# Grouping of the output projection's passes, the ring of raw tiles and the order of the first MLP unit in a hybrid attention and RWKV-7 encoder layer

## The chip, the cores and the metric

The kernel runs on one core of a Trainium2 chip. The core has five engines with an instruction stream each: TensorE (PE, matrix products; its weight loads are listed as PEld), VectorE (DVE), ScalarE (ACT), GpSimd (POOL) and SyncE (SP, which here issues DMA transfers). They wait for one another by semaphores. The metric is the time on the device in microseconds, as the median of several executions.

## What is computed

One encoder layer on x of 1024 positions by 1024 features in float32. The change lies behind the attention and the RWKV part, in the last two lines:

```python
x = x + jnp.concatenate([attn, rwkv], axis=-1) @ w_out[layer]
h = _rms_norm(x, ln2_g[layer])
x = x + jnp.square(jax.nn.relu(h @ w_up[layer])) @ w_down[layer]
```

`w_out` is 1024 x 1024, `w_up` 1024 x 4096 and `w_down` 4096 x 1024.

## The kernel before, in words

All of it stands in `tail`. Data lies with features on the 128 partitions and positions along the free axis, so x is eight tiles `x1[c]` of 128 x 1024, and a half `hf` of one is 128 x 512. Float32 products are made of three matmuls: each operand is split into a high part (a cast by ACT) and a low part (a subtraction by DVE), in `split_w` (L101, L102), and `mm3` (L105, L106, L107) issues high times high, high times low and low times high into one PSUM tile.

**Output projection.** `w_out(ks, c)` loads the weight blocks of column block c for the input tiles ks (`w2raw`), splits them (`w2h`, `w2l`), and for both halves runs three matmuls for each tile of ks and adds the result to x1[c] on DVE (L1026). Input tiles 4 to 7 are RWKV outputs (`rw`), 0 to 3 attention outputs (`f`). Tile 3 is written in place by the last attention pair, while tiles 0 to 2 are loaded back by `cat` from DRAM (`catr`) and split. There are three passes over the eight column blocks: [4, 5, 6, 7], interleaved with the last pieces of attention, then [0, 1], then [2, 3].

**Making h.** Inside the last pass each finished x1[c] becomes `hraw` (L1059, ACT). The norm's scale by position is applied later, after the up layer. The up layer multiplies 2 x 2 blocks with seven products in place of eight, so that for each pair of column blocks seven quadrants are made, 11, 21, 22 as they are and T1 to T4 from differences `ht` (L1067, L1068, L1071, L1072), each split into a high (L1056, ACT) and a low part (L1057, DVE).

**Up layer.** Sixteen units of two w_up tiles (`wuraw`, 512 KB each). `factors` forms the seven weight combinations, with sums on POOL (`wus`, L1099), and splits each (`wuh`, `wul`); `up_unit` runs a product of twelve matmuls for each and adds outputs on DVE (L1152). `sums` squares x1 on ACT (L1120, `sqt`) and adds on POOL (L1121) into `rep`; `scales` turns that into the norm's factor through PE (`psr`, L1126), a square root on ACT, a reciprocal on DVE and PE again (`psb`, L1132); `finish` applies factor, relu and square (L1168, L1169) and stores to `f_dr` (L1170).

**Down layer.** Four groups of eight `f_dr` tiles, each loaded in halves (`fraw`) and split (`mh`, `ml`); for each column block the weights (`wdraw`, two of 256 KB) are split (`wdh`, `wdl`), and 48 matmuls follow.

**What sets the order.** A scheduler orders the instructions of each engine by a priority that grows along the code, while every tile pool gives out a fixed number of buffers, and a tile that takes an old buffer's place waits until its readers are done. `ahead(n)` lets pieces of code take an earlier priority: the attention pieces of `some(4)` are such. On every engine instructions run strictly in the order so made.

## Time and profile before

| | us |
|---|---|
| median of 3 runs | 1776.54 |
| lowest, highest | 1776.28, 1782.05 |
| the profiled execution | 1780.65 |
| its span, first to last instruction | 1778.6 |
| output projection, from its first matmul (979.85) to its last | 95 |
| from there to the first matmul of unit 1 | 55 |
| units 1 to 15 | 286 |
| down layer with its start | 358 |

The profile is of one execution, so its times are set against its own 1780.65 us. A page lists busy time by engine, groups of like instructions with the mean of one, and what ended the idle time ahead of them; a timeline lists single instructions with start and length in microseconds; a table of windows gives busy time and count for each engine in stretches of time.

### The profile page before, as it was taken

The numbers are of one execution on the slowest core, as the hardware profiler recorded it, in microseconds if no ns is written. First come the engines' busy times: TensorE is split into PE (matmuls) and PEld (weight loads), VectorE is DVE, ScalarE is ACT, GpSimd is POOL, SyncE is SP. The second block draws the span as 40 slices with busy tenths as digits, with TensorE's granted clock in tenths as the row PEclk, the third lists the DMA queues.
The fourth block names the chain that finished last, engine by engine and source line by source line (L and its number), as shares of the span: only waits on it lengthen the run. The fifth ranks groups of instructions, "written<-read, shape, count | busy, mean of one in ns | idle before, by whom it ended". The sixth has DMA issues, their size and how long they took to land.

```text
span 1778.6 us, 30157 instructions
## 1 busy us (share of the span) xinstructions
PE 1622.7 (91%) x11720; PEld 1342.5 (75%) x11720; DVE 1031.8 (58%) x1946; ACT 596.9 (34%) x1091; POOL 424.5 (24%) x462
## 2 busy tenths in 40 slices
PE   7999978979869998988998994999999899999999
PEld 5777767767757777877786883888888788888887
DVE  6655657747545323565776578778878662424221
ACT  5544333443412213434465336222222251212110
POOL 3022022222200000221223117766666500000000
PEclk9999988879889997888998996999999999999999
DMA  6155787889875598998873411232232381413121
GB/s 220 46 143 129 155 166 154 174 178 187 190 172 142 170 231 194 270 264 228 228 219 108 155 36 36 83 131 101 103 128 101 105 268 49 141 63 110 48 96 52
DMA packets 347805, 256.67 MB, mean 144 GB/s; under 512 B 239984, under 2 KB 293120, under 8 KB 343568
## 3 DMA queue, kind: packets, MB, share of 16 engines
q1 hardware_dynamic: 311280, 212.60, 46.0%
q0 software_dynamic: 8704, 26.78, 5.0%
q10 hardware_dynamic: 27680, 15.38, 3.3%
q8 instruction: 92, 1.51, 0.4%
q14 instruction: 49, 0.40, 0.1%
HBM read 167.00 MB, written 87.69 MB: 143 GB/s over the span
## 4 chain that ended last, share of the span: by engine, by line
PE 67%; DMA 13%; DVE 9%; SPq 4%; issue 3%; ACT 3%; POOL 1%; ACTq 0%; DVEq 0%; POOLq 0%
PE ps L105 13%; PE ps L107 13%; PE ps L106 13%; PE ps_u L107 3%; PE ps_u L106 3%; PE ps_u L105 3%; DMA v_dr<-vn 2%; PE pvb L748 2%; DMA rec_dr<-G 2%; PE psd L564 2%; PE psg L496 1%; DMA ql<-ql_dr 1%; PE ps_pt L742 1%; DMA rec<-rec_dr 1%; DMA t<-td 1%
## 5 line engine op out<-in xcount | busy, mean ns | idle before, releaser
L105 PE MATMUL ps<-mh,wdh 128*128 128x512 f32 x512 | 199.5, 391 | 6.8 <-ACT wdh L101 6.8
L106 PE MATMUL ps<-ml,wdh 128*128 128x512 f32 x512 | 200.0, 391 | 0.0
L107 PE MATMUL ps<-mh,wdl 128*128 128x512 f32 x512 | 199.5, 391 | 0.0
L105 PE MATMUL ps_u<-hh,wh 128*128 128x512 f32 x368 | 156.3, 425 | 3.5 <-DVE ur L308 3.5
L107 PE MATMUL ps_u<-hh,wl 128*128 128x512 f32 x368 | 151.4, 411 | 0.0
L106 PE MATMUL ps_u<-hl,wh 128*128 128x512 f32 x368 | 150.7, 410 | 0.0
L1204 DVE TENSOR_TENSOR x<-x,ps 128x512 f32<-128x512 f32 x64 | 43.9, 686 | 150.0 <-PE ps L107 150.0
L105 PEld LDWEIGHTS ps<-mh,wdh 128*128 128x128 f32 x512 | 96.8, 189 | 27.2 <-ACT wdh L101 7.2
L107 PEld LDWEIGHTS ps<-mh,wdl 128*128 128x128 f32 x512 | 96.7, 189 | 20.3
L101 ACT CAST wdh<-wdraw 128x512 fp32r<-128x512 f32 x64 | 39.7, 622 | 215.3 <-PE ps L106 209.7
L106 PEld LDWEIGHTS ps<-ml,wdh 128*128 128x128 f32 x512 | 96.7, 189 | 20.0
L105 PEld LDWEIGHTS ps_u<-hh,wh 128*128 128x128 f32 x368 | 72.5, 197 | 20.2 <-DVE ur L308 4.3
L107 PEld LDWEIGHTS ps_u<-hh,wl 128*128 128x128 f32 x368 | 72.3, 197 | 17.7 <-issue 1.6
L106 PEld LDWEIGHTS ps_u<-hl,wh 128*128 128x128 f32 x368 | 72.2, 196 | 16.3 <-issue 2.4
L101 ACT CAST wuh<-wus 128x512 fp32r<-128x512 f32 x64 | 39.6, 622 | 128.9 <-PE ps L106 120.3
L102 DVE TENSOR_TENSOR wdl<-wdraw,wdh 128x512 fp32r<-128x512 f32 x64 | 44.0, 688 | 57.4 <-ACT wdh L101 57.3
L102 DVE TENSOR_TENSOR wul<-wus,wuh 128x512 fp32r<-128x512 f32 x64 | 67.9, 1062 | 12.1 <-ACT wuh L101 10.5
L496 PE MATMUL psg<-al,bk 64*128 64x128 f32 x512 | 56.8, 318 | 19.2 <-DVE G L501 10.6
L496 PEld LDWEIGHTS psg<-al,bk 64*128 64x128 f32 x512 | 48.0, 216 | 26.9 <-issue 11.9
L705 DVE CUSTOM_DVE_ANT_0 sb<-ps_s,bias 128x256 f32<-128x256 f32 (+1 forms) x136 | 50.0, 403 | 30.6 <-PE ps_pt L719 24.6
L1169 POOL TENSOR_TENSOR zz<-zz 128x512 f32<-128x512 f32 x48 | 57.4, 1195 | 35.3 <-DVE zz L1168 35.3
L102 DVE TENSOR_TENSOR wul<-wuraw,wuh 128x512 fp32r<-128x512 f32 x48 | 61.3, 1277 | 3.5 <-ACT wuh L101 1.9
(408 smaller groups left out, 4045.7 us busy)
## 6 DMA issues: line engine op xcount, KB each, us to landing
...
wuraw<-in_w_up SPq DMA_DIRECT2D x32, 512.0 KB, 4.2
fraw<-f_dr SPq DMA_DIRECT2D x64, 256.0 KB, 3.7
wdraw<-in_w_dn SPq DMA_DIRECT2D x64, 256.0 KB, 2.5
f_dr<-zz POOLq DMA_DIRECT2D x48, 256.0 KB, 2.5
raw<-in_w_in SPq DMA_DIRECT2D x46, 256.0 KB, 3.1
...
rec_dr<-G SPq DMA_DIRECT2D x32, 256.0 KB, 4.4
```

What stands on the lines that cost most here:

```text
L101: nc.scalar.copy(hi, raw)
L102: nc.vector.tensor_sub(lo, raw, r2f(hi))
L105: nc.tensor.matmul(ps, lh, rh, start=start, stop=False)
L106: nc.tensor.matmul(ps, lh, rl, start=False, stop=False)
L107: nc.tensor.matmul(ps, ll, rh, start=False, stop=stop)
L496: nc.tensor.matmul(pss[h][:, c], bk[H[h], 4 * g + c, h:h + 2].rearrange("p a b -> p (a b)"), al[H[h], 4 * g + c].rearrange("p a b -> p (a ...
L564: nc.tensor.matmul(ps[H[h], c], L[H[h], c], R[H[h], c], start=True, stop=True)
L705: nc.vector.tensor_tensor_reduce(sb[rows, i, :n], ps[rows, i, cols], b[rows], -1.0, 3.0e38, ALU.add, ALU.min, O[rows, js][:, i, mc:mc + 1])
L742: nc.tensor.transpose(pt[:, x, i * P:(i + 1) * P], sb[:, i, x * P:(x + 1) * P], ident)
L748: nc.tensor.matmul(pv[:, i], pts[:, x, i * P:(i + 1) * P], vB[:, x * 4 + c], start=(x == 0), stop=(x == 1))
L1169: nc.gpsimd.tensor_mul(t, t, t)
L1204: nc.vector.tensor_add(x1[c][:, HS[hf]], x1[c][:, HS[hf]], ps)
```

## The change

The passes become [4, 5, 6, 7], [0] and [1, 2, 3]: the middle one has half the matmuls that it had and the last one half as many again. All raw tiles of 128 x 1024 (attention tiles, w_up, f_dr, w_down) come from one ring `raw4` of two buffers, three from the up layer on, and the split weights of both MLP layers from one pool `wu` that lasts. The first two w_up tiles are loaded before the last pass. t2 is made by POOL instead of DVE, and the differences have two buffers instead of three. Unit 0 takes its products in the order 11, 21, 22, T2, T3, T1, T4; every other unit keeps 11, T2, T3, T1, 21, T4, 22. `sums` stands behind unit 0 in the code, with half of its additions on DVE, and the weights of the down layer's first column block are loaded and split ahead of that layer. Line numbers behind the change are some 11 to 31 higher.

```diff
+            wr = st.enter_context(tc.tile_pool(name="wr", bufs=2, side="right", reuse_waits="tile"))
             out = ExitStack()
-            c23 = out.enter_context(tc.tile_pool(name="c23", bufs=1, side="right", reuse_waits="tile"))
-            wp = out.enter_context(tc.tile_pool(name="wp3", bufs=4, side="right", reuse_waits="tile"))
+            c13 = out.enter_context(tc.tile_pool(name="c13", bufs=1, side="right", reuse_waits="tile"))
+            wp = out.enter_context(tc.tile_pool(name="wp3", bufs=2, side="right", reuse_waits="tile"))
+            wp.tile([P, 384], F32, name="rest4", bufs=1)
...
-            parts = [[c01.tile([P, S], F32R, name=f"f{i}{k}") for k in range(2)] +
-                     [c23.tile([P, S], F32R, name=f"f{i}{k}") for k in (2, 3)] +
+            o0 = ExitStack()
+            c00 = o0.enter_context(tc.tile_pool(name="c00", bufs=1, side="right", reuse_waits="tile"))
+            w0 = o0.enter_context(tc.tile_pool(name="w0", bufs=3, side="right", reuse_waits="tile"))
+            parts = [[(c13 if k else c00).tile([P, S], F32R, name=f"f{i}{k}") for k in range(4)] +
                      [rw[i][:, p] for p in range(4)] for i in range(2)]
             fh, fl = parts
+            pools, turn = [(wr, "raw4")] * 2, [0]
+
+            def raw4(src):
+                pool, tag = pools[turn[0] % len(pools)]
+                turn[0] += 1
+                r = pool.tile([P, NK, P], F32, name="raw4", tag=tag)
+                nc.sync.dma_start(r, src)
+                return r
...
+                raw = raw4(cat_dr[k].rearrange("p (k m) -> p k m", m=P)).rearrange("p k m -> p (k m)")
                 for hf in range(2):
-                    raw = wp.tile([P, 512], F32, name="catr", bufs=2)
-                    nc.sync.dma_start(raw, cat_dr[k][:, HS[hf]])
-                    split_w(raw, fh[k][:, HS[hf]], fl[k][:, HS[hf]])
-
-            def w_out(ks, c):
-                ws = []
-                for k in ks[::2]:
-                    raw = wp.tile([P, 2, P], F32, name="w2raw")
-                    nc.sync.dma_start(raw, w_o[c][:, k:k + 2])
-                    ws.append([wp.tile([P, 2, P], F32R, name=n) for n in ("w2h", "w2l")])
-                    split_w(raw, *ws[-1])
+                    split_w(raw[:, HS[hf]], fh[k][:, HS[hf]], fl[k][:, HS[hf]])
...
+            def w_out(wp, ks, c):
+                ws = {}
+                for i in range(0, len(ks), 3 if len(ks) == 3 else 2):
+                    k = ks[i]
+                    n = len(ks) if len(ks) < 4 else 2
+                    raw = wp.tile([P, n, P], F32, name="w2raw", bufs=3)
+                    nc.sync.dma_start(raw, w_o[c][:, k:k + n])
+                    w = [wp.tile([P, n, P], F32R, name=x) for x in ("w2h", "w2l")]
+                    split_w(raw, *w)
...
-                w_out([4, 5, 6, 7], c)
+                w_out(w0, [4, 5, 6, 7], c)
...
-                w_out([0, 1], c)
-            o01.close()
+                w_out(w0, [0], c)
...
-            rep = hp.tile([P, S], F32, name="rep3")
+            raws = {f: raw4(w_up[f]) for f in (0, 1)}
             with tc.tile_pool(name="ht", bufs=2, side="right", reuse_waits="tile") as ht:
                 for c in range(NK):
-                    w_out([2, 3], c)
+                    w_out(wp, [1, 2, 3], c)
...
-                    t1, t2, t3, t4 = (ht.tile([P, 512], F32, name=f"ht{i}", tag="ht", bufs=3) for i in range(4))
+                    t1, t2, t3, t4 = (ht.tile([P, 512], F32, name=f"ht{i}", tag="ht") for i in range(4))
                     nc.gpsimd.tensor_sub(t1, he[:, HS[1]], he[:, HS[0]])
-                    nc.vector.tensor_sub(t2, h[:, HS[1]], t1)
+                    nc.gpsimd.tensor_sub(t2, h[:, HS[1]], t1)
...
-            wu = up_.enter_context(tc.tile_pool(name="wu", bufs=4, side="right", reuse_waits="tile"))
+            wu = st.enter_context(tc.tile_pool(name="wu", bufs=4, side="right", reuse_waits="tile"))
+            wr3 = st.enter_context(tc.tile_pool(name="wr3", bufs=1, side="right", reuse_waits="tile"))
+            pools.append((wr3, "raw5"))
+            zu = up_.enter_context(tc.tile_pool(name="zu", bufs=5, side="right", reuse_waits="tile"))
+            rep = zu.tile([P, S], F32, name="rep3", bufs=1)
...
-                    r = wu.tile([P, NK, P], F32, name="wuraw", bufs=3)
-                    nc.sync.dma_start(r, w_up[f])
+                    r = raws.pop(f) if f in raws else raw4(w_up[f])
...
+                yield halves(a11)
+                if u == 0:
+                    yield halves(a12)
                 s1 = summed(nc.gpsimd.tensor_add, a21, a22)
                 s2 = summed(nc.gpsimd.tensor_sub, s1, a11)
-                yield parts(s2)
-                yield parts(summed(nc.gpsimd.tensor_sub, a11, a21))
-                yield parts(s1)
-                yield parts(a12)
-                yield parts(a22)
-                yield parts(summed(nc.gpsimd.tensor_sub, a12, s2))
+                if u == 0:
+                    yield halves(summed(nc.gpsimd.tensor_sub, a12, s2))
+                yield halves(s2)
+                yield halves(summed(nc.gpsimd.tensor_sub, a11, a21))
+                yield halves(s1)
+                if u > 0:
+                    yield halves(a12)
+                yield halves(a22)
+                if u > 0:
+                    yield halves(summed(nc.gpsimd.tensor_sub, a12, s2))
 
...
-                        t = wu.tile([P, 512], F32, name="sqt", tag="z")
+                        t = zu.tile([P, 512], F32, name="sqt", tag="z")
                         nc.scalar.activation(t, x1[c][:, sl], AF.Square)
-                        nc.gpsimd.tensor_add(rep[:, sl], rep[:, sl], t)
+                        (nc.gpsimd if hf else nc.vector).tensor_add(rep[:, sl], rep[:, sl], t)
...
+                if u == 0:
+                    z11, = add([t1], "21", [z("z")])
+                    p3 = acc()
+                    prod(p3, "22")
+                    c3 = z("z")
+                    nc.scalar.copy(c3, p3)
                 U2, = add([t1], "T2", [z("u", bufs=1)])
                 U3, = add([U2], "T3", [z("t3", bufs=1)])
                 z22, V = add([U3, U2], "T1", [z("z"), z("z")])
-                z11, = add([t1], "21", [t1])
-                z21, = add([U3], "T4", [z("z")])
-                z12, = add([V], "22", [V])
+                if u > 0:
+                    z11, = add([t1], "21", [t1])
+                z21, = add([U3], "T4", [z("z") if u else U3])
+                if u > 0:
+                    z12, = add([V], "22", [V])
+                else:
+                    z12 = V
+                    nc.vector.tensor_add(V, V, c3)
...
+            first = up_unit(0)
             sums()
-            first = up_unit(0)
             scales()
...
+            def dn(g, c):
+                r = raw4(w_dn[g, c])
+                return [halves(r[:, 4 * j:4 * j + 4]) for j in range(2)]
+            ws = dn(0, 0)
             up_.close()
...
-            wd = st.enter_context(tc.tile_pool(name="wd", bufs=4, side="right", reuse_waits="tile"))
...
+                    raw = raw4(f_dr[g * 8 + f].rearrange("p (k m) -> p k m", m=P)).rearrange("p k m -> p (k m)")
                     for hf in range(2):
-                        raw = wd.tile([P, 512], F32, name="fraw")
-                        nc.sync.dma_start(raw, f_dr[g * 8 + f][:, HS[hf]])
-                        split_w(raw, hi[:, HS[hf]], lo[:, HS[hf]])
+                        split_w(raw[:, HS[hf]], hi[:, HS[hf]], lo[:, HS[hf]])
...
-                    ws = []
-                    for j in range(2):
-                        raw = wd.tile([P, 4, P], F32, name="wdraw")
-                        nc.sync.dma_start(raw, w_dn[g, c][:, 4 * j:4 * j + 4])
-                        ws.append([wd.tile([P, 4, P], F32R, name=n) for n in ("wdh", "wdl")])
-                        split_w(raw, *ws[-1])
+                    if g + c:
+                        ws = dn(g, c)
```

On SP, the stretch that ends in the loads of x1, before (cat_dr_91 is attention tile 2 in DRAM):

```order
L1018 DMA w2raw<-in_w_o 128x256 x4
L1011 DMA catr<-cat_dr_89 128x512 x2
L1018 DMA w2raw<-in_w_o 128x256 x4
L836 DMA cat_dr_91<-aT 128x512
L896 DMA bon<-bon_dr 128x4x128
L895 DMA gt<-g_dr 128x4x128
L836 DMA cat_dr_91<-aT 128x448
L836 DMA cat_dr_91<-aT 128x64
L1030 DMA x_0_10313<-in_xT 128x1024
```

and now:

```order
L1010 DMA raw_10712<-cat_dr_89 128x1024
L1010 DMA raw_10718<-cat_dr_90 128x1024
L836 DMA cat_dr_91<-aT 128x512
L896 DMA bon<-bon_dr 128x4x128
L895 DMA gt<-g_dr 128x4x128
L836 DMA cat_dr_91<-aT 128x448
L836 DMA cat_dr_91<-aT 128x64
L1010 DMA raw_10724<-cat_dr_91 128x1024
L1010 DMA raw_10922<-in_w_up 128x1024
L1029 DMA w2raw<-in_w_o 128x256 x3
L1029 DMA w2raw<-in_w_o 128x384
L1042 DMA x_0_10313<-in_xT 128x1024
```

The eight early loads of w2raw moved behind the load of attention tile 2 and that of the first w_up tile.

On ACT, from the last h quadrant to the norm's square root, before (wuh are weights of units 0 and 1):

```order
L1056 CAST hT4h_10955<-ht_11239 128x512
L1120 ACTIVATE sqt<-x_1_10314 128x512 x2
L1120 ACTIVATE sqt<-x_2_10315 128x512 x2
L1120 ACTIVATE sqt<-x_3_10316 128x512
L101 CAST wuh<-wuraw 128x512
L1120 ACTIVATE sqt<-x_3_10316 128x512
L1120 ACTIVATE sqt<-x_4_10317 128x512 x2
L1120 ACTIVATE sqt<-x_5_10318 128x512
L1157 COPY zt<-ps_11338 128x512
L1120 ACTIVATE sqt<-x_5_10318 128x512
L101 CAST wuh<-wus 128x512 x3
```

and now, where the casts of a11 and a12 stand further up:

```order
L1068 CAST hT4h_10909<-ht_11244 128x512
L1178 COPY zt<-ps_11306 128x512
L1138 ACTIVATE rep_11273<-x_0_10313 128x512 x2
L101 CAST wuh<-wus 128x512 x4
L101 CAST wuh<-raw_10924 128x512
L1184 COPY zz<-ps_11344 128x512
L101 CAST wuh<-raw_11529 128x512
L101 CAST wuh<-wus 128x512 x2
L1141 ACTIVATE sqt<-x_1_10314 128x512
L101 CAST wuh<-wus 128x512
L1141 ACTIVATE sqt<-x_1_10314 128x512
L1141 ACTIVATE sqt<-x_2_10315 128x512 x2
```

The squares moved from ahead of unit 0's weights to behind all of them and four of unit 1's.

On DVE, from the last output of the up layer into the down layer, before:

```order
L1152 TENSOR_TENSOR zz<-zz,ps_13841 128x512
L1168 SCALAR_TENSOR_TENSOR zz<-zz,rep_10968 128x512
L102 TENSOR_TENSOR ml_13882<-fraw,mh_13881 128x512 x2
L102 TENSOR_TENSOR ml_13892<-fraw,mh_13891 128x512 x2
L102 TENSOR_TENSOR wdl<-wdraw,wdh 128x512 x3
L102 TENSOR_TENSOR ml_13902<-fraw,mh_13901 128x512
L102 TENSOR_TENSOR wdl<-wdraw,wdh 128x512
```

and now:

```order
L1173 TENSOR_TENSOR zt<-zt,ps_13814 128x512
L102 TENSOR_TENSOR wul<-raw_13883,wuh 128x512
L1200 SCALAR_TENSOR_TENSOR zt<-zt,rep_11273 128x512
L1173 TENSOR_TENSOR zz<-zt_13772,ps_13833 128x512
L1200 SCALAR_TENSOR_TENSOR zz<-zz,rep_11273 128x512
L1173 TENSOR_TENSOR zz<-zz,ps_13851 128x512
L1200 SCALAR_TENSOR_TENSOR zz<-zz,rep_11273 128x512
L102 TENSOR_TENSOR ml_13899<-raw_13900,mh_13898 128x512 x2
L102 TENSOR_TENSOR ml_13907<-raw_13908,mh_13906 128x512 x2
```

The low part of the first down weights moved into the last unit, while the low parts of all f tiles stay behind its last output.

More of the change, by code (lines that the diff above doesn't have):

```diff
@@ L1008, in cat @@
             def cat(k):
+                raw = raw4(cat_dr[k].rearrange("p (k m) -> p k m", m=P)).rearrange("p k m -> p (k m)")
                 for hf in range(2):
[L1010 to L1020 removed]
+                    split_w(raw[:, HS[hf]], fh[k][:, HS[hf]], fl[k][:, HS[hf]])
[8 more added lines that the diff above has]
+                    split_w(raw, *w)
+                    for z in range(n):
+                        ws[k + z] = w[0][:, z], w[1][:, z]
                 for hf in range(2):
@@ L1023, in w_out @@
                     for i, k in enumerate(ks):
[L1024 to L1025 removed]
+                        mm3(ps, *ws[k], fh[k][:, HS[hf]], fl[k][:, HS[hf]], i == 0, i == len(ks) - 1)
                     nc.vector.tensor_add(x1[c][:, HS[hf]], x1[c][:, HS[hf]], ps)
@@ L1036, in tail @@
             for c in range(NK):
-                w_out([0, 1], c)
-            o01.close()
+                w_out(w0, [0], c)
+            o0.close()
             left.close()
@@ L1079, in acc, with halves @@
                 return pu.tile([P, 512], F32, name=name, tag="acc")
-            wu = up_.enter_context(tc.tile_pool(name="wu", bufs=4, side="right", reuse_waits="tile"))
+            wu = st.enter_context(tc.tile_pool(name="wu", bufs=4, side="right", reuse_waits="tile"))
[3 more added lines that the diff above has]
+            rep = zu.tile([P, S], F32, name="rep3", bufs=1)
             f_dr = [dr.tile([P, S], F32, name=f"f_dr{f}") for f in range(32)]
+            def halves(src):
+                w = [wu.tile([P, 4, P], F32R, name=n) for n in ("wuh", "wul")]
+                split_w(src, *w)
+                return w
             def factors(u):
@@ L1086, in factors @@
                 for f in (2 * u, 2 * u + 1):
-                    r = wu.tile([P, NK, P], F32, name="wuraw", bufs=3)
-                    nc.sync.dma_start(r, w_up[f])
+                    r = raws.pop(f) if f in raws else raw4(w_up[f])
                     raw.append(r.rearrange("p (k e) m -> p e k m", e=2))
                 a11, a12, a21, a22 = raw[0][:, 0], raw[0][:, 1], raw[1][:, 0], raw[1][:, 1]
-                def parts(src):
-                    w = [wu.tile([P, 4, P], F32R, name=n) for n in ("wuh", "wul")]
-                    split_w(src, *w)
-                    return w
                 def summed(fn, x, z):
-                    t = wu.tile([P, 4, P], F32, name="wus", bufs=3)
+                    t = zu.tile([P, 4, P], F32, name="wus", bufs=3)
                     fn(t, x, z)
                     return t
-                yield parts(a11)
+                yield halves(a11)
+                if u == 0:
+                    yield halves(a12)
                 s1 = summed(nc.gpsimd.tensor_add, a21, a22)
                 s2 = summed(nc.gpsimd.tensor_sub, s1, a11)
-                yield parts(s2)
-                yield parts(summed(nc.gpsimd.tensor_sub, a11, a21))
-                yield parts(s1)
-                yield parts(a12)
-                yield parts(a22)
-                yield parts(summed(nc.gpsimd.tensor_sub, a12, s2))
+                if u == 0:
[8 more added lines that the diff above has]
+                    yield halves(summed(nc.gpsimd.tensor_sub, a12, s2))
             def sums():
@@ L1145, in z @@
                 def z(tag, **kw):
-                    return wu.tile([P, 512], F32, name=f"z{tag}", tag=tag, **kw)
+                    return zu.tile([P, 512], F32, name=f"z{tag}", tag=tag, **kw)
                 def add(a, q, out):
```

4 lines of the change are left out of this document (removed).

## The prediction

> **What bounds the kernel now.** I read the first part of the page and its costliest groups first, then a table of windows over the last 800 us, then the timeline at the idle places that the table shows.
>
> ```profile
> PE 1622.7 (91%) x11720; PEld 1342.5 (75%) x11720; DVE 1031.8 (58%) x1946; ACT 596.9 (34%) x1091; POOL 424.5 (24%) x462
> ...
> 979.30:1008.00 28.70, 28.70 (x159) 24.61 (x158) 16.43 (x35) 10.12 (x25) 0.00 (x0) 1.00 0.51 179
> ...
> 1057.30:1075.30 18.00, 17.75 (x74) 13.02 (x72) 17.68 (x26) 13.88 (x23) 8.67 (x6) 1.00 0.01 1
> 1075.30:1096.20 20.90, 0.12 (x1) 0.00 (x0) 19.62 (x23) 13.59 (x23) 12.53 (x9) 0.56 0.09 27
> 1096.20:1131.00 34.80, 29.30 (x117) 23.57 (x118) 20.18 (x22) 13.31 (x22) 28.65 (x21) 0.79 0.17 60
> 1131.00:1417.20 286.20, 286.20 (x1260) 236.65 (x1259) 226.10 (x268) 70.83 (x117) 183.19 (x181) 1.00 0.31 108
> 1417.20:1424.00 6.80, 0.05 (x1) 0.00 (x0) 3.99 (x6) 2.47 (x4) 2.57 (x3) 0.88 0.82 255
> 1424.00:1431.00 7.00, 6.95 (x20) 5.60 (x21) 5.34 (x8) 4.30 (x8) 0.00 (x0) 0.63 1.02 375
> 1431.00:1778.60 347.60, 343.89 (x1518) 284.51 (x1516) 117.93 (x180) 69.75 (x116) 0.00 (x0) 1.00 0.30 98
> ```
>
> Columns: length, then busy time and count of PE, PEld, DVE, ACT, POOL, then granted clock, DMA share and GB/s. PE is full in every stage that the change touches but two: 21 us after the output projection, where DVE is busy for 19.6 of 20.9, with a slow first unit behind it, and 7 us ahead of the down layer, where the DMA share is 0.82. Only those two places have something to give. In between, 1260 matmuls in 286.2 us, the first few of them slow, make 0.2267 us each: a product of 12 is 2.72 us, a unit of 84 is 19.0.
>
> ```profile
> 1075.02 0.40 PE L107 MATMUL ps<-f,w2l 128*128 128x512 f32 x1
> ...
> 1092.12 3.63 SPq L1088 DMA_DIRECT2D wuraw<-in_w_up  x3
> ...
> 1093.16 1.76 DVE L1057 TENSOR_TENSOR hT4l<-ht,hT4h 128x512 fp32r<-128x512 f32 x1
> ...
> 1095.56 0.62 ACT L101 CAST wuh<-wuraw 128x512 fp32r<-128x512 f32 x1 [0.53 <-DMA wuraw<-in_w_up]
> ...
> 1096.23 0.80 PE L105 MATMUL ps<-h11h,wuh 128*128 128x512 f32 x1 [20.81 <-ACT wuh L101]
> ...
> 1122.70 0.39 PE L107 MATMUL ps<-h22h,wul 128*128 128x512 f32 x1
> ...
> 1122.93 1.84 PE L1126 MATMUL psr<-ct,rep 128*128 128x2 f32 x16
> ...
> 1127.16 3.78 PE L1132 MATMUL psb<-ct,rstd 128*128 128x128 f32 x16 [2.40 <-DVE rstd L111]
> ...
> 1130.60 0.77 PE L105 MATMUL ps<-h11h,wuh 128*128 128x512 f32 x1
> ```
>
> Call W = 1075.25 the end of the last w_out matmul. The last h split ends at 1094.92, W + 19.7; the load of the first w_up tile goes out only at 1092.12, its cast is at 1095.56, unit 0 runs from 1096.23 to 1122.93 (26.7 us for 19.0 of work), the norm's chain psr, rstd, psb takes 7.7 us more, and **unit 1 starts at W + 55.35**. I forecast when unit 1 starts after the change, since sixteen units and the norm lie behind it in either kernel.
>
> **The first transition.**
>
> ```profile
> L1026 DVE TENSOR_TENSOR x<-x,ps 128x512 f32<-128x512 f32 x16 | 10.7, 678 | 2.0 <-PE ps L107 2.0
> L1057 DVE TENSOR_TENSOR h22l<-hraw,h22h 128x512 fp32r<-128x512 f32 x4 | 4.3, 1071 | 0.0
> ...
> L1068 DVE TENSOR_TENSOR ht<-hraw,ht 128x512 f32<-128x512 f32 x4 | 3.8, 955 | 0.0
> ...
> L1057 DVE TENSOR_TENSOR hT3l<-ht,hT3h 128x512 fp32r<-128x512 f32 x4 | 2.7, 678 | 0.0
> L1121 POOL TENSOR_TENSOR rep<-rep,sqt 128x512 f32<-128x512 f32 x14 | 21.1, 1534 | 1.3 <-ACT sqt L1120 1.3
> ...
> L1099 POOL TENSOR_TENSOR wus<-wus,wuraw 128x512 f32<-128x512 f32 x2 | 2.5, 1272 | 0.0
> L1120 ACT ACTIVATE sqt<-x 128x512 f32<-128x512 f32 x14 | 8.5, 627 | 8.1 <-POOL rep L1121 8.1
> 1083.02 1.64 POOL L1072 TENSOR_TENSOR ht<-hraw,ht 128x512 f32<-128x512 f32 x1 [2.43 <-DVE hT1l L1057]
> 1083.47 1.74 DVE L1057 TENSOR_TENSOR hT2l<-ht,hT2h 128x512 fp32r<-128x512 f32 x1
> ```
>
> The last pass has 18 matmuls for each column block instead of 12, 4.08 us instead of 2.72, so it covers 10.9 us more of the same h work. DVE also loses four t2 subtractions (3.8 us). Of the 19.7 us that it lagged behind W some 8 to 9 remain by that, and I take W + 11, since POOL now has four steps in a pair's chain and each hands over to a split on DVE.
>
> That handing over is where a rule bears on it. A split that began 0.45 us after a POOL subtraction took 1.74 us, against 0.68 free. The Trainium skill, page "SBUF — State Buffer", section "Who interferes with whom", says that a DVE instruction with two SBUF inputs and a GpSimd one that reads SBUF exclude each other for the whole instruction; the trace agrees, since that split ends 0.55 us after POOL is done, while the PSUM adds stay at 678 ns. By that rule a moved t2 gives back what it frees; by counts alone the lag would be W + 8.
>
> With both w_up tiles loaded in advance, the cast of a11 waits for the last w_out matmul only: products 11 and 21 start at about W + 2.3. The third product needs a12 − s2, which is the sixth POOL operation after the last x add (t2, t3, t4, s1, s2, the difference, 1.27 to 1.53 us each, with two handovers): from W + 5 that is about W + 15.7, with the cast W + 16.4. PE idles there for some 8 us. Five products (13.6 us) and the low clock after the idle time (2 us) end **unit 0 at W + 32**, 15.7 us earlier than before.
>
> The gain does not reach unit 1. The squares and sums now stand behind unit 0's own casts: on ACT the second of 14 squares comes after a cast that waits for the product T4, unit 0's last, and the tiles that they rotate through are down to two, as the other three hold outputs of unit 0 until the norm is known. A pair, one added by DVE and one by POOL, costs 2 × (0.63 + 0.68 to 1.53) us on each tile in turn, about 1.9 us for a pair with both tiles in use; 7 pairs from W + 32.4 end at about W + 46. The second half of psr, rstd and psb follow (6.9 of the 7.7 us). **Unit 1 starts at about W + 53: a gain of 2.5 us**, bounds −10 (the POOL chain not late) and +3 (2.3 us a pair).
>
> **Ahead of the first pass.**
>
> ```profile
> 942.44 2.31 SPq L1018 DMA_DIRECT2D w2raw<-in_w_o  x4
> 958.19 2.07 SPq L1018 DMA_DIRECT2D w2raw<-in_w_o  x4
> ...
> 970.24 12.58 SPq L1030 DMA_DIRECT2D x<-in_xT  x8
> ...
> 974.07 1.28 ACT L708 ACT_TABLE_LOAD   x1
> ...
> 979.85 0.71 PE L105 MATMUL ps<-rw,w2h 128*128 128x512 f32 x2
> ...
> x<-in_xT SPq DMA_DIRECT2D x8, 512.0 KB, 7.9
> ...
> wuraw<-in_w_up SPq DMA_DIRECT2D x32, 512.0 KB, 4.2
> fraw<-f_dr SPq DMA_DIRECT2D x64, 256.0 KB, 3.7
> ```
>
> Eight w2raw loads lay ready 20 us early. Now none is issued until the w_up load ahead of them on SP has a buffer, that is after cat 2 has been stored, loaded again (some 4 us) and split. The two casts of cat 2 stand before ACT's table load as well: it moves from 974.07 to about 977.4, and with it the attention softmax behind it. The w2h casts come behind the casts of cat 0; I get the first w_out matmul at 986.8 instead of 979.85. From 979.3 on PE was full with attention and w_out interleaved, so of the 7 us those 3.4 are not lost in which attention pieces now run earlier: **a loss of 4**, bounds 1 (all attention pulled forward) and 8 (nothing). Pass [0] gives PE 1.36 us a column block against two adds and a split of 1.5 us on DVE: +0.5, bounds 0 and 2.
>
> **The down layer.**
>
> ```profile
> 1417.06 1.28 SPq L1189 DMA_DIRECT2D fraw<-f_dr  x3
> ...
> 1423.38 0.62 ACT L101 CAST wdh<-wdraw 128x512 fp32r<-128x512 f32 x1
> ...
> 1424.05 0.80 PE L105 MATMUL ps<-mh,wdh 128*128 128x512 f32 x1 [6.80 <-ACT wdh L101]
> ```
>
> Now the first load waits for memory of the up layer. The down layer runs from 1417.25 (1424.05 less the 6.80 idle) to 1774.89 (1431.00 and 343.89 busy), 357.6 us for 1536 matmuls that need 348.2 at 0.2267: 9.4 too many. After the change f0, f1, f2 and the weights come early, but their low parts stand on DVE behind the last up outputs (E + 1.7, E the end of unit 15), and f3 to f7 each wait for a buffer of three: eight tiles ready at about E + 2, 4, 5, 9, 10, 11.5, 15 and 16.5, the group's first column block done at E + 17.3 where 10.9 is pure. PE has no second block between, as it had before. Excess 7.3: **a gain of 2.1**, bounds −7 and +2. At the first change of groups, f8 to f15 and the next weights pass through the same three buffers, each waiting for a split; by replay with 4.2 us a load they are ready 2 us late, **a loss of 3** with the clock's drop, bounds 0 and 8 (all three changes late). The idle 2.4 us ahead of psb were enough for slow matmuls: 0.77 us at 1130.60, against 0.39 at 1122.70. The Trainium skill, page "TensorE: Matmul & The Clock Gate", section "What's actually happening", asks for an idle window of about 3.4 us; by that the loss would be 2, which the trace does not support.
>
> **Sum**: 4 + 0.5 − 2.5 − 2.1 + 3 = +2.9 us. The profiled execution took 1780.65 us, 4.11 above the median of 1776.54, so 1783.6 for it and **1779 us** as a median. Its unknowns alone make 1770 to 1788. A measurement of this kernel can tell about 0.3% (5.3 us) from no change.
>
> **Rivals.** *Both gaps close*: POOL keeps up in the last pass, so that the third product does not wait (−7), and the boundary stays covered (−3); 1769 us. For it speaks that DVE alone was full in the 21 us, POOL 12.5 of 20.9; against it, that the sums end last whatever unit 0 does. *Three buffers are too few*: a load of 512 KB that takes 5.4 us, a third of the way from the 4.2 of w_up to the 7.9 of the eight x loads in a row, adds 1.2 us to each of some four serial steps at every change of groups. That is 5 us at each of three, 12 more than I sum: 1789 us, slower. It decides where a column block's 10.9 us no longer cover two loads with their splits (2 × 5.4). For it speaks the DMA share of 1.02 at 1424; against it 0.30 afterwards. *The change does not do what it says*: the early loads stay behind waits on SP, unit 0 begins as late as before: +2.5 more, 1782.
>
> **How the numbers follow.** Forecast 0.5, gaps close 0.25, ring too small 0.17, no early loads 0.08. Faster: the second and a tenth of the first, 0.3. Slower: ring, and a fifth of the forecast and half of the last, 0.3. Same 0.4. The range leaves a tenth on each side: 1764 to 1790.
>
> **What would show it.** First w_out matmul near 987 and the table load near 977; unit 0 ended by W + 32, then some 14 us in which PE waits for rep at psr; unit 1 at W + 53; at the down layer short waits for mh and ml instead of one of 7 us; about 2 us idle at the first change of groups. If PE does not wait at psr, the time is below 1771; if w_out starts by 981, 3 us fall away.

## The result, and the profile after

| | before | after |
|---|---|---|
| median, us | 1781.9 (7 runs) | 1793.06 (7 runs) |
| lowest, highest | 1776.28, 1788.4 | 1788.32, 1798.4 |
| after / before | | 1.0071, interval 1.0046 to 1.0096 |
| the profiled execution, its span | 1780.65, 1778.6 | 1798.4, 1796.5 |

The change makes the kernel **slower by 0.7%**: the ratio is that of the means, 12.6 us apart, and the medians are 11.2 us apart. The forecast was 1779, with 1764 to 1790 as the range: the time lies 3 us above it. The busy times of the page of after have hardly moved:

```profile
PE 1630.6 (91%) x11720; PEld 1346.6 (75%) x11720; DVE 1030.1 (57%) x1949; ACT 595.8 (33%) x1092; POOL 420.4 (23%) x459
```

The table of windows of before, cut at the first w_out matmul, the last one (W), and the end of unit 0 (columns as in the prediction):

```profile
959.81:979.85 20.04, 16.33 (x101) 14.38 (x102) 9.56 (x37) 11.95 (x24) 2.55 (x2) 0.74 0.41 126
979.85:1075.25 95.40, 95.14 (x447) 77.86 (x445) 64.88 (x117) 34.26 (x73) 16.62 (x13) 1.00 0.27 89
1075.25:1122.93 47.68, 23.80 (x86) 17.98 (x86) 33.98 (x37) 24.26 (x40) 39.26 (x27) 0.71 0.16 55
```

The same of after, with the wait for the sums, the norm, units 1 to 15, the down layer's first column block and its rest as windows of their own:

```profile
963.45:994.94 31.49, 23.65 (x125) 21.27 (x126) 14.47 (x50) 17.20 (x36) 2.54 (x2) 0.67 0.28 84
994.94:1087.34 92.40, 91.89 (x423) 75.62 (x421) 65.88 (x114) 32.75 (x67) 23.25 (x18) 1.00 0.30 104
1087.34:1122.75 35.41, 25.40 (x85) 19.27 (x84) 24.28 (x31) 15.76 (x27) 18.79 (x14) 0.81 0.14 45
1122.75:1138.96 16.21, 0.16 (x1) 0.03 (x1) 10.51 (x9) 7.71 (x14) 9.27 (x7) 0.59 0.00 0
1138.96:1146.85 7.89, 7.15 (x33) 6.98 (x33) 1.50 (x3) 2.07 (x3) 1.27 (x1) 0.50 0.01 2
1146.85:1433.83 286.98, 286.98 (x1263) 237.51 (x1263) 226.71 (x271) 73.53 (x122) 183.12 (x181) 1.00 0.33 114
1433.83:1453.13 19.30, 13.68 (x49) 8.28 (x47) 12.18 (x19) 7.51 (x14) 2.58 (x4) 1.00 0.64 224
1453.13:1796.50 343.37, 338.14 (x1488) 279.05 (x1488) 112.18 (x174) 63.76 (x109) 0.00 (x0) 1.00 0.29 94
```

Both tables start at the first matmul of the last RWKV block's sum of squares (L124 of before), called base here. The 13 profiles of this study reach it anywhere from 951.0 to 964.4 us, although PE runs the same 8264 matmuls ahead of it, so intervals are counted from it. From base to W the kernel takes 123.89 us instead of 115.44 (+8.45). From W to unit 1 it takes 59.51 (35.41 + 16.21 + 7.89) instead of 55.35 (+4.16): unit 0 ends 12.3 us earlier, and then PE does almost nothing for 16.21 us. Units 1 to 15 take 286.98 instead of 286.50 (+0.48). The down layer, the idle time ahead of it counted in, takes 358.30 instead of 357.64 (+0.66). The sum is +13.75, against +12.6 by the means of the timed runs; each profile is of one execution, and that of after (1798.4) is the slowest of its seven.

The stretch from base to W as one window, in before, after, e1 and e6 (two of the experiments below):

```profile
959.81:1075.25 115.44, 111.48 (x545) 92.24 (x545) 74.44 (x154) 46.20 (x95) 19.16 (x15) 0.96 0.29 96
963.45:1087.34 123.89, 115.54 (x545) 96.90 (x545) 80.36 (x163) 49.95 (x101) 25.79 (x20) 0.92 0.29 99
960.33:1078.08 117.75, 113.36 (x545) 94.27 (x545) 79.43 (x161) 49.80 (x99) 25.80 (x20) 0.94 0.30 99
956.74:1072.39 115.65, 111.16 (x545) 92.34 (x545) 79.41 (x161) 49.75 (x99) 25.76 (x20) 0.96 0.30 101
```

PE runs the same 545 matmuls in each. Of the 8.45 us that after takes longer than before, 4.4 are idle time (8.35 instead of 3.96), and 4.1 are longer busy time (115.54 instead of 111.48) at a granted clock of 0.92 instead of 0.96.

Ahead of W, the timeline of after (start, length, instruction; in brackets the idle time before it and what ended it):

```profile
982.01 1.14 ACT L101 CAST f<-raw 128x512 fp32r<-128x512 f32 x2 [2.45 <-DMA raw<-cat_dr]
983.17 1.28 ACT L708 ACT_TABLE_LOAD   x1
984.50 0.33 SPq L1010 DMA_DIRECT2D raw<-in_w_up  x1
984.89 8.42 SPq L1029 DMA_DIRECT2D w2raw<-in_w_o  x4
985.46 0.47 PE L727 MATMUL pv<-vA,pts 128*128 128x65 f32 x2 [2.65 <-ACT OA L732]
991.79 0.41 PE L702 MATMUL ps_s<-kko,qlo 128*128 128x256 f32 x1
992.25 1.14 ACT L101 CAST f<-raw 128x512 fp32r<-128x512 f32 x2 [1.08 <-PE ps_s L702]
994.26 1.00 ACT L101 CAST w2h<-w2raw 128x256 fp32r<-128x256 f32 x3
994.94 0.48 PE L105 MATMUL ps<-rw,w2h 128*128 128x512 f32 x1
```

Two things are late. ACT waits 2.45 us for attention tile 2, the table load stands behind its casts, and PE waits 2.65 us for ACT. And SP, once past the w_up load at 984.50, spends 8.42 us on four w2raw loads: behind the first of them it sits until the matmul of 991.79 is done. That is an attention score product, which has nothing to do with w_out but for the memory that it reads. The cast of an attention tile at 992.25, which stands ahead of the first w2h casts on ACT, waits 1.08 us for the same matmul. PE itself does not idle ahead of its first w_out matmul (994.94): attention pieces stand there in its order.

Behind W:

```profile
1091.26 0.57 PE L105 MATMUL ps<-h11h,wuh 128*128 128x512 f32 x1 [3.75 <-ACT wuh L101]
...
1095.05 1.57 POOL L1080 TENSOR_TENSOR ht<-hraw,ht 128x512 f32<-128x512 f32 x1 [1.92 <-DVE hT4l L1069]
...
1100.13 1.27 POOL L1084 TENSOR_TENSOR ht<-hraw,ht 128x512 f32<-128x512 f32 x1 [1.83 <-DVE hT3l L1069]
...
1102.09 1.08 DVE L1069 TENSOR_TENSOR hT4l<-ht,hT4h 128x512 fp32r<-128x512 f32 x1 [2.04 <-ACT hT4h L1068]
...
1105.67 1.14 ACT L101 CAST wuh<-wus 128x512 fp32r<-128x512 f32 x2 [2.08 <-POOL wus L1114]
1106.35 0.80 PE L105 MATMUL ps<-h22h,wuh 128*128 128x512 f32 x1 [5.62 <-ACT wuh L101]
...
1133.62 1.15 ACT L1141 ACTIVATE sqt<-x 128x512 f32<-128x512 f32 x2 [1.47 <-DVE rep L1142]
1134.39 1.26 POOL L1142 TENSOR_TENSOR rep<-rep,sqt 128x512 f32<-128x512 f32 x1 [1.35 <-ACT sqt L1141]
1134.80 1.40 DVE L1142 TENSOR_TENSOR rep<-rep,sqt 128x512 f32<-128x512 f32 x1 [1.21 <-ACT sqt L1141]
1136.23 1.15 ACT L1141 ACTIVATE sqt<-x 128x512 f32<-128x512 f32 x2 [1.47 <-DVE rep L1142]
...
1138.96 3.85 PE L1147 MATMUL psr<-ct,rep 128*128 128x2 f32 x16 [16.06 <-DVE rep L1142]
1139.62 1.27 POOL L1142 TENSOR_TENSOR rep<-rep,sqt 128x512 f32<-128x512 f32 x1 [1.35 <-ACT sqt L1141]
```

Unit 0 begins 3.9 us after W (20.98 before), its third product waits for the POOL difference, and psr waits 16.06 us for the sums. In that POOL chain t2 (1095.05) and t4 (1100.13) wait 1.92 and 1.83 us for low parts on DVE. Neither reads what DVE made, so these are waits for one of the buffers of the differences, of which the change leaves two. A pair of squares comes every 2.61 us (1133.62 to 1136.23): the two squares take 1.15, and then ACT waits 1.47 for the buffer that a DVE addition holds. The two additions of a pair do not run freely side by side: the DVE one takes 1.40 us and ends 0.55 us after POOL's.

### The profile page after: what moved, and what is told of

Same layout as the page of the kernel before. It is cut to its first block, busy times and chain, and to the rows that moved or that the text cites. A ratio compares the mean times of both kernels' runs of the same rounds, so it can differ in the third digit from the quotient of the medians.

```text
span 1796.5 us, 29980 instructions
## 1 busy us (share of the span) xinstructions
PE 1630.6 (91%) x11720; PEld 1346.6 (75%) x11720; DVE 1030.1 (57%) x1949; ACT 595.8 (33%) x1092; POOL 420.4 (23%) x459
## 4 chain that ended last, share of the span: by engine, by line
PE 63%; DMA 14%; DVE 11%; SPq 5%; ACT 4%; issue 3%; POOL 1%; ACTq 0%; DVEq 0%; POOLq 0%
PE ps L105 12%; PE ps L106 12%; PE ps L107 12%; PE ps_u L105 3%; PE ps_u L106 3%; PE ps_u L107 3%; DMA v_dr<-vn 2%; PE pvb L748 2%; PE psd L564 2%; PE psg L496 2%; DMA rec<-rec_dr 1%; DMA raw<-f_dr 1%; PE ps_pt L742 1%; DVE stmp L534 1%; DMA MP<-gd 1%
## 5 line engine op out<-in xcount | busy, mean ns | idle before, releaser
L105 PE MATMUL ps<-mh,wuh 128*128 128x512 f32 x512 | 199.6, 391 | 4.5 <-ACT mh L101 3.2
L106 PE MATMUL ps<-ml,wuh 128*128 128x512 f32 x512 | 199.8, 390 | 2.1 <-DVE ml L102 2.1
L107 PE MATMUL ps<-mh,wul 128*128 128x512 f32 x512 | 199.2, 389 | 0.0
L101 ACT CAST wuh<-raw 128x512 fp32r<-128x512 f32 x112 | 68.9, 622 | 284.7 <-PE ps L106 276.1
L102 DVE TENSOR_TENSOR wul<-raw,wuh 128x512 fp32r<-128x512 f32 x112 | 104.7, 938 | 55.1 <-ACT wuh L101 53.6
L105 PEld LDWEIGHTS ps<-mh,wuh 128*128 128x128 f32 x512 | 96.1, 188 | 27.2 <-ACT mh L101 5.5
L106 PEld LDWEIGHTS ps<-ml,wuh 128*128 128x128 f32 x512 | 96.1, 188 | 23.7 <-DVE ml L102 3.8
L107 PEld LDWEIGHTS ps<-mh,wul 128*128 128x128 f32 x512 | 96.1, 188 | 19.9 <-DVE wul L102 0.4
L102 DVE TENSOR_TENSOR ml<-raw,mh 128x512 fp32r<-128x512 f32 x64 | 42.5, 700 | 62.7 <-ACT mh L101 62.7
L102 DVE TENSOR_TENSOR wul<-wus,wuh 128x512 fp32r<-128x512 f32 x64 | 63.7, 998 | 4.4 <-ACT wuh L101 4.4
```

The source lines that it names most:

```text
L101: nc.scalar.copy(hi, raw)
L102: nc.vector.tensor_sub(lo, raw, r2f(hi))
L105: nc.tensor.matmul(ps, lh, rh, start=start, stop=False)
L106: nc.tensor.matmul(ps, lh, rl, start=False, stop=False)
L107: nc.tensor.matmul(ps, ll, rh, start=False, stop=stop)
```

## The experiments

Each kernel is the changed one with the edit shown. All the intervals, in us, each from one profile, with the timed median of the runs beside them ("end" is the start of the last matmul of the down layer; a row "x = y + z" has the edits of y and z). The medians come from several chips. The runs of before beside them have a median of 1780.86 (e1 to e4), 1779.44 (e5 to e8), 1777.03 (e9) and 1780.24 (e10, e11), and a ratio to before is taken against these:

| kernel | base to first w_out | base to W | W to end of unit 0 | W to unit 1 | down layer | base to end | median (runs) |
|---|---|---|---|---|---|---|---|
| before | 20.04 | 115.44 | 47.68 | 55.35 | 357.64 | 814.69 | 1781.9 (7) |
| after | 31.49 | 123.89 | 35.41 | 59.51 | 358.30 | 828.45 | 1793.06 (7) |
| e1 weights near | 22.27 | 117.75 | 34.25 | 58.33 | 358.30 | 820.54 | 1791.91 (5) |
| e2 cat halves | 32.25 | 123.06 | 34.04 | 58.11 | 358.51 | 825.74 | 1792.59 (1) |
| e3 sums on DVE | 30.96 | 123.39 | 35.55 | 54.25 | 357.07 | 820.91 | 1786.06 (10) |
| e4 sums on POOL | 30.85 | 123.32 | 34.95 | 59.86 | 357.63 | 826.99 | 1796.96 (1) |
| e5 sums first | 31.78 | 124.35 | 41.03 | 46.10 | 358.36 | 815.12 | 1783.58 (1) |
| e6 = e1 + e3 + e5 | 20.03 | 115.65 | 37.51 | 43.75 | 357.08 | 803.24 | 1767.82 (6) |
| e7 passes undone | 34.10 | 126.73 | 43.82 | 67.90 | 356.75 | 837.55 | 1807.27 (1) |
| e8 t2 on DVE | 31.24 | 123.15 | 36.06 | 60.13 | 358.28 | 828.26 | 1794.46 (1) |
| e9 = e6 + a raw buffer | 20.42 | 117.36 | 38.06 | 43.59 | 353.13 | 799.94 | 1764.15 (6) |
| e10 = e3 + e5 | 31.07 | 123.58 | 37.87 | 42.14 | 356.79 | 808.01 | 1773.7 (12) |
| e11 = e6 again | 20.24 | 117.30 | 38.21 | 43.62 | 356.90 | 803.79 | 1768.41 (11) |

**Ahead of W: the weights' memory or attention tile 2?** In e1 the w_out weights get the pool that is opened first:

```diff
-            c13 = out.enter_context(tc.tile_pool(name="c13", bufs=1, side="right", reuse_waits="tile"))
             wp = out.enter_context(tc.tile_pool(name="wp3", bufs=2, side="right", reuse_waits="tile"))
             wp.tile([P, 384], F32, name="rest4", bufs=1)
+            c13 = out.enter_context(tc.tile_pool(name="c13", bufs=1, side="right", reuse_waits="tile"))
...
-            w0 = o0.enter_context(tc.tile_pool(name="w0", bufs=3, side="right", reuse_waits="tile"))
...
-                w_out(w0, [4, 5, 6, 7], c)
+                w_out(wp, [4, 5, 6, 7], c)
...
-                w_out(w0, [0], c)
+                w_out(wp, [0], c)
```

The edit also gives the first two passes two buffers of each split weight tile instead of three, and it moves the place of the attention tiles' pool `c13`.

> The pool of the output projection's weights lies ahead of the attention tiles' pool again and serves all three passes (two buffers of each split tile instead of three), everything else as in the changed kernel. From the first matmul that sums the last RWKV block's squares (psb, L124) to the last w_out matmul the kernel before took 115.4 us and the changed one 123.9. Theory A, the weights' buffers lie on memory that the last attention pair still reads, so the loads wait: the interval returns to 115 to 118 us, and the median falls by 6 to 9 us to about 1785. Theory B, the loads are late only because ACT and SP wait for attention tile 2 in front of them: the interval stays above 121.

In e2 the attention tiles come in halves again:

```diff
-                raw = raw4(cat_dr[k].rearrange("p (k m) -> p k m", m=P)).rearrange("p k m -> p (k m)")
...
-                    split_w(raw[:, HS[hf]], fh[k][:, HS[hf]], fl[k][:, HS[hf]])
+                    raw = wr.tile([P, 512], F32, name="catr", tag="raw4")
+                    nc.sync.dma_start(raw, cat_dr[k][:, HS[hf]])
+                    split_w(raw, fh[k][:, HS[hf]], fl[k][:, HS[hf]])
```

> The attention tiles 0 to 2 are loaded in halves through the two ring buffers, so that tile 2 and the first w_up tile come behind the loads of x1, while the weights' pool stays where the change put it. Theory A (memory of the weights' pool): the second weight load still waits for the last score matmuls of attention, first w_out matmul late, interval from the sum of squares of the last RWKV block to the last w_out matmul 121 us or more. Theory B (tile 2 in front of ACT's table load and the weights on SP): back to about 116.

SP's queue in the timeline of e1:

```profile
941.88 2.47 SPq L1028 DMA_DIRECT2D w2raw<-in_w_o  x3
...
958.71 0.81 SPq L1028 DMA_DIRECT2D w2raw<-in_w_o  x2
...
970.78 14.56 SPq L1041 DMA_DIRECT2D x<-in_xT  x8
```

and in that of e6, which has the same edit ahead of W:

```profile
967.12 12.64 SPq L1041 DMA_DIRECT2D x<-in_xT  x8
979.86 0.39 SPq L1009 DMA_DIRECT2D raw<-cat_dr  x1
```

The weight loads stand where they stood before the change, and 6.1 of the 8.45 us are back (117.75). The pool's place moves the memory and, with it, SP's order, in which the load of attention tile 2 now comes behind those of x as well (979.86). So these kernels do not part the memory from tile 2. The median of e1, 1.1 us below that of after, does not resolve the gain, though base to end is 7.9 shorter. So e10 and e11 ask again, on one chip, with the edits of e3 and e5, which are described further down:

```diff
 e10: the edits of e3 and e5
 e11: the edits of e1, e3 and e5
```

> e6 without its first edit: additions on DVE and sums ahead of unit 0, the weights' pool of the output projection where the change put it. Run beside e6 on the same chip. Theory A (the late buffers of these weights cost 6 to 8 us): the interval from the last RWKV block's sum of squares to the last w_out matmul is 123 to 124.5 us against 115.7 in e6, unit 1 starts 43 to 45 us after that matmul in both, and the median is 5 to 8 us above e6's. Rival, the gain of the near pool is lost elsewhere, as the medians of e1 (2 us below the changed kernel) would say: the two medians are within 3 us.

> The kernel of e6 again, on the same chip as e10. Theory A: the interval to the last w_out matmul is 115 to 117 us, median 5 to 8 us below that of e10. Rival: within 3 us of it.

Base to W is 123.58 without e1's edit and 117.30 with it, and the medians 1773.7 and 1768.4: 5.3 us (the means differ by 4.6), where 6.3 are measured in the interval. Against before (1780.24) e10 is at 0.9971 (0.9954 to 0.9987), e11 at 0.994 (0.9917 to 0.9963). In e2, with the pool where the change put it, base to W is still 123.06. Tile 2 comes behind the x loads there, so its place is not all of the loss. It does not show the memory's share either, since its w2raw loads got behind six x loads on SP (first w_out matmul at 32.25). By e1's edit the profiles fall into two groups: base to W is 115.65 to 117.75 us in the four with it, and 123.06 to 124.35 in after and the others but e7.

**Behind W: the additions' engine, or the sums' place?** e3 puts all 14 additions on DVE, e4 on POOL:

```diff
-                        (nc.gpsimd if hf else nc.vector).tensor_add(rep[:, sl], rep[:, sl], t)
+                        nc.vector.tensor_add(rep[:, sl], rep[:, sl], t)
```

> All fourteen additions of the squares on DVE, none on POOL, the rest as in the changed kernel, where a pair of additions (one DVE, one POOL) took 2.61 us and psr began 51.6 us after the last w_out matmul, unit 1 59.5 us after it. Theory lock: a DVE addition waits for the POOL addition beside it, so that a pair costs about what both cost in a row; on DVE alone an addition takes 0.68 us, a pair 1.3 to 1.5, psr begins 43 to 45 us after the last w_out matmul and unit 1 at 51 to 53; the median falls by 7 to 9 us to about 1785. Rival, the two rotating buffers and the squares on ACT set the pace: a pair stays at 2.3 us or more and the median within 3 us of 1793.

> All fourteen additions of the squares on POOL, none on DVE, the rest as in the changed kernel. Theory lock: an undisturbed POOL addition takes 1.27 us, so a pair takes 2.5 to 2.6 us, the same as with half of them on DVE, and unit 1 starts 59 to 60 us after the last w_out matmul as before. Rival, DVE and POOL really work side by side: a pair takes over 3 us and unit 1 starts at 62 or later.

The group of these additions (busy, mean ns of one, idle before it and what ended it), in after:

```profile
L1142 POOL TENSOR_TENSOR rep<-rep,sqt 128x512 f32<-128x512 f32 x7 | 9.4, 1348 | 7.6 <-ACT sqt L1141 7.5
L1142 DVE TENSOR_TENSOR rep<-rep,sqt 128x512 f32<-128x512 f32 x7 | 7.9, 1134 | 5.6 <-ACT sqt L1141 5.6
```

in e3:

```profile
L1142 DVE TENSOR_TENSOR rep<-rep,sqt 128x512 f32<-128x512 f32 x14 | 9.1, 687 | 0.6
```

and in e4:

```profile
L1142 POOL TENSOR_TENSOR rep<-rep,sqt 128x512 f32<-128x512 f32 x14 | 17.7, 1310 | 3.8 <-ACT sqt L1141 3.8
```

From the first addition's start to the last one's end it takes 18.9 us in after (1122.03 to 1140.89), 12.5 in e3 (1122.57 to 1135.06) and 19.9 in e4 (1120.11 to 1140.06). Once the squares follow one another, a pair comes every 2.61 us in after, 1.38 in e3 and 2.44 in e4. So half of the additions on DVE make a pair no shorter than all of them on POOL. e3 brings unit 1 forward by 5.3 us, a little less than expected, and to 1786.06 (ratio to before 1.0041, 1.0021 to 1.006); in e4 unit 1 stays where it was.

e5 leaves the two engines and moves the sums ahead of unit 0 in the code:

```diff
-            first = up_unit(0)
             sums()
+            first = up_unit(0)
```

> Only the call of sums is put back ahead of unit 0 in the code, with half of the additions on DVE and half on POOL as in the changed kernel; so its squares and additions stand between the last h splits and unit 0's later weights. Theory place: unit 0 ends some 3 us later (38 to 40 us after the last w_out matmul instead of 35.4), but psr follows at once, and unit 1 starts at 46 to 48 instead of 59.5: about 12 us gained from the last w_out matmul on. Rival, DVE and POOL are the limit in the whole stretch, so that the additions only push unit 0 away: unit 1 starts at 56 or later.

Unit 0 ends 5.6 us later than in after, but psr no longer waits, and unit 1 comes at W + 46.10, 13.4 earlier. The place costs more than the choice of engine.

In e5 the squares run before unit 0's outputs hold any of the five tiles that both share, where in after three are held. The timeline of DVE there:

```profile
1102.55 7.93 DVE L1142 TENSOR_TENSOR rep<-rep,sqt 128x512 f32<-128x512 f32 x5 [0.48 <-ACT sqt L1141]
```

With POOL working beside it, an addition on DVE takes 1.59 us here, against 0.69 in e3. So the two engines slow each other here too, but ACT waits at most 0.55 us for a tile, not 1.47 for each pair as in after. How much of the 2.61 us is the two engines and how much the two tiles is not parted: no run gave the squares of after more tiles.

Together, with e1's edit, in e6:

> Three edits together: the weights' pool ahead of the attention tiles, all additions of the squares on DVE, and sums ahead of unit 0 in the code. If the costs are those that the single edits show (6 us before the last w_out matmul; unit 1 at 44 to 46 us after it instead of 59.5), the time from the last RWKV block's sum of squares to the last matmul falls from 828 us to 805 to 810, below the 814.7 of the kernel before, and the median to 1773 to 1778, faster than before by 0.2 to 0.5 per cent. If the additions between the splits and the weights cost unit 0 as much as psr gains, it stays at 813 or more and the median at that of before or above.

The timeline of e6:

```profile
1093.43 0.80 PE L105 MATMUL ps<-h22h,wuh 128*128 128x512 f32 x1 [8.63 <-ACT wuh L101]
...
1109.90 1.84 PE L1146 MATMUL psr<-ct,rep 128*128 128x2 f32 x16
```

PE waits for nothing at psr, and the sums lie in the 8.63 us in which it waits for the third product's weights. e6 took 1767.82, a ratio to before of 0.9939 (0.992 to 0.9959): faster than both kernels, and 5 us below the range that was expected.

**The longer last pass and t2.** e7 splits the passes as before the change:

```diff
-            parts = [[(c13 if k else c00).tile([P, S], F32R, name=f"f{i}{k}") for k in range(4)] +
+            parts = [[(c13 if k > 1 else c00).tile([P, S], F32R, name=f"f{i}{k}") for k in range(4)] +
-                w_out(w0, [0], c)
+                w_out(w0, [0, 1], c)
-                    w_out(wp, [1, 2, 3], c)
+                    w_out(wp, [2, 3], c)
```

> The passes are again [4, 5, 6, 7], [0, 1], [2, 3], all else as in the changed kernel. Theory cover: the last pass is 10.9 us shorter, so the h splits end that much later after the last w_out matmul, unit 0 ends at 43 to 46 us after it instead of 35.4, and unit 1, behind the sums, at 67 to 70 instead of 59.5. Rival, only the early w_up loads and the order of the products shorten the start of unit 0: unit 1 at 60 to 63.

Unit 0 ends 8.4 us later and unit 1 comes at W + 67.90: the cover of the longer pass is real. Base to W grew by 2.8 as well, which I had not expected; the first w_out matmul is later, in a layout where the weights' pool lies elsewhere again. Five weight loads go out there before base or just behind it (960.05 to 966.05), and yet the matmul comes at 34.10: early loads alone do not bring it forward.

e8 gives t2 back to DVE:

```diff
-                    nc.gpsimd.tensor_sub(t2, h[:, HS[1]], t1)
+                    nc.vector.tensor_sub(t2, h[:, HS[1]], t1)
```

> Only the four subtractions t2 are put back on DVE. Theory lock (DVE and POOL exclude each other, so moving t2 to POOL frees nothing on DVE and lengthens POOL's chain): unit 0's third product waits 1 to 2 us less and unit 0 ends 33 to 34.5 us after the last w_out matmul instead of 35.4. Rival, DVE's backlog is what is late: unit 0 ends 2 us later or more.

Neither theory's change came: unit 0 ends at W + 36.06, and base to end is 828.26 against 828.45. The engine of t2 is worth nothing that shows.

**The ring of raw tiles.** e9 is e6 with one more buffer from the down layer on:

```diff
+            wr4 = st.enter_context(tc.tile_pool(name="wr4", bufs=1, side="right", reuse_waits="tile"))
+            pools.append((wr4, "raw6"))
```

> The three edits of e6 and a fourth buffer in the ring of raw tiles from the down layer on (the memory that the up layer leaves). Theory ring: the f tiles of the down layer's start and of the first change of groups wait for a buffer, so the fourth takes 2 to 4 us off the down layer, from 357 to 358 us (last unit's end to last matmul, 348.2 of them matmuls) to 354 or 355, and the short wait at the first change of groups goes; the median falls to 1764 to 1766. Rival, the low parts of the f tiles on DVE, behind the up layer's last outputs, or the transfers themselves set the pace: the down layer stays at 357 or more.

The group of the down layer's products that wait for the high parts, in e6 (count, busy, mean ns, idle before them and what ended it):

```profile
L105 PE MATMUL ps<-mh,wuh 128*128 128x512 f32 x512 | 200.0, 391 | 2.8 <-ACT mh L101 1.9 <-ACT wuh L101 0.7
```

and in e9:

```profile
L105 PE MATMUL ps<-mh,wuh 128*128 128x512 f32 x512 | 199.3, 390 | 1.0 <-ACT mh L101 1.0
```

The waits for weights are gone and those for f tiles halved. The layer takes 353.13 us, 4.0 less than in e6 (357.08). Of these, 3.3 lie in the first column block: 15.85 us (1398.05 to 1413.90) instead of 19.12 (1403.13 to 1422.25). This group's idle time is a poor measure of it: in e10, with three buffers, it is 1.2, and the layer takes 356.79. e9 took **1764.15**, a ratio of 0.9924 (0.9896 to 0.9952) to before; the two ratios alone do not tell it from e6.

## Why the prediction was wrong

| term of the sum | forecast | measured |
|---|---|---|
| ahead of W, with pass [0] | +4.5 | +8.45 |
| W to unit 1 | -2.5 | +4.16 |
| units 1 to 15 | 0 | +0.48 |
| down layer | -2.1 + 3 | +0.66 |
| sum | +2.9 | +13.75 |

The timed runs differ by 11.2 us in their medians and by 12.6 in their means, so the terms account for the miss; that the median of before rose from 1776.54 (3 runs) to 1781.9 (7) is a further 5 us that the change has no part in.

**Ahead of W: the step "behind the w_up load" stopped one wait too early.** The order on SP was right: w_up at 984.50 and w2raw behind it. I took the loads to go out there, and put the first w_out matmul 7 us later; it came 11.45 later. The table load came 5.5 us later where 3.3 were forecast (983.17 and 974.07, each counted from base). The term left out is the memory: the first pass's weights got a pool of their own at a place that the last attention pair still reads. e1, and e10 against e11, show that 6 us hang on where this pool lies. How they come about is shown only in part. SP's wait is in the trace, but the pool's place also moves tile 2 in SP's order, and half of the 8.45 us is longer busy time at a lower granted clock. The forecast has no term for that: the stretch up to the first w_out matmul, where the last attention pieces run without w_out's matmuls among them, is 11.45 us longer, at 0.67 instead of 0.74. The recovery came out near its size: 92.40 instead of 95.40 to W, 3.0 against the forecast 3.4. That is partly luck, since it was reckoned for a delay of 7 us. What is left with the near pool is 0.2 us in e6 and 2.3 in e1, which have the same code up to W, so single profiles scatter by that much. Pass [0] cost 0.1 to 1.7 us: from the first w_out matmul to W it is 95.48 in e1, 95.62 in e6, 97.06 in e11 and 95.40 before, where +0.5 was forecast.

**First transition: the mechanism held, its sizes did not.** Products 11 and 21 begin at W + 3.9 (forecast 2.3), PE waits for the third product's difference and then for the sums at psr, 16 us where I said some 14. Two terms were short. The third product started at W + 19.0 (forecast 16.4), and unit 0 ended at 35.4 instead of 32. t2 is not the reason (e8). The POOL chain waits twice for DVE, 1.92 and 1.83 us, where the third buffer of the differences, which the change takes away, is priced at nothing in the forecast. Such a wait stands in before too (2.43 us at 1083.02, in the prediction's lines), and no run gave the third buffer back, so this cause is argued. The last h split ended at W + 15.8, forecast W + 11. The counts given there, 19.7 less 10.9 and 3.8, make 5.0 and not the 8 to 9 that stand beside them, but the sum does not use them. The larger term is the pair of sums: 2.61 us where I took 1.9 and, as my bound for the worst, 2.3. I laid the squares and the additions of the two tiles side by side, 0.63 + 0.68 to 1.53. In the trace two squares, 1.15 us, are followed by a wait of 1.47 us for an addition on DVE that takes 1.40 us, twice its time in e3. In the same section I had shown a split that waits for a POOL subtraction. The rule of the Trainium skill, page "SBUF — State Buffer", section "Who interferes with whom", is that two such instructions exclude each other. It agrees with this trace, where the DVE addition ends 0.55 us after POOL's. I had applied it to t2, where e8 shows no effect, and not to the sums. The 4.1 us that the additions took beyond my 14 and the 3.4 of unit 0, less 1.0 by which the end of the norm's chain was shorter, make the 6.6 between -2.5 and +4.16.

The prediction had the place of the sums in its chain, as the reason why the gain doesn't reach unit 1, with 14 us from the end of unit 0. What it costs against the old place e5 shows: unit 1 comes 13.4 us earlier by that edit alone, with the 5.6 of a later unit 0 already in that.

**Down layer: right in sum, by two errors that offset each other.** Short waits stand in place of one of 6.8 us. The timeline of PE in after:

```profile
1433.83 0.61 PE L105 MATMUL ps<-mh,wuh 128*128 128x512 f32 x2
1436.09 0.50 PE L106 MATMUL ps<-ml,wuh 128*128 128x512 f32 x1 [1.65 <-DVE ml L102]
...
1442.18 1.02 PE L105 MATMUL ps<-mh,wuh 128*128 128x512 f32 x2 [1.39 <-ACT mh L101]
...
1445.37 1.02 PE L105 MATMUL ps<-mh,wuh 128*128 128x512 f32 x2 [1.13 <-ACT mh L101]
...
1453.13 0.50 PE L105 MATMUL ps<-mh,wuh 128*128 128x512 f32 x1 [0.23 <-ACT wuh L101]
...
1530.60 0.50 PE L105 MATMUL ps<-mh,wuh 128*128 128x512 f32 x1 [1.01 <-ACT wuh L101]
```

The first column block takes 19.30 us where 10.88 is pure: an excess of 8.4, forecast 7.3 (the 17.3 and 10.9 given there make 6.4). All that follows costs 1.7 us, forecast 3. The wait at the first change of groups (1530.60) is 1.0 us, forecast 2 with slow matmuls behind it. No slow ones came: a matmul takes 0.50 there, and the granted clock of both down windows is 1.00. So the wait of 2.40 us, from which I argued that the clock would drop, was no guide to that change of groups. Why not is open: its waits are shorter, and the 2.40 stood behind the 16 narrow matmuls of psr. Short waits do not always leave the clock alone. In e10 a wait of 1.65 us at the start of the same layer is followed, within 2 us, by a stretch at half clock with matmuls of 0.63 us:

```profile
1418.31:1421.72 3.41, 3.41 (x10) 2.63 (x9) 1.91 (x4) 0.00 (x0) 0.00 (x0) 0.50 0.88 282
```

The Trainium skill, page "TensorE: Matmul & The Clock Gate", section "What's actually happening", asks for an idle window of about 3.4 us. By that the prediction had 2 in place of 3, which was nearer for after; the stretch in e10, which no wait of 3.4 us precedes, does not fit it.

**Rivals.** The time came out 4 us above "three buffers are too few" (1789; its own 12 on 1779 would be 1791), for another reason: one buffer more is worth 4.0 us over the whole layer (e9 against e6), where 12 were counted at the changes of groups alone. "Both gaps close" failed as its counter-argument said, on the sums. "No early loads" did not occur: unit 0 began 3.9 us after W.
